# Separate buffers for block 2's background norms, their sums issued late, and GpSimd's weight remainders in four pieces

## The chip, the cores and the metric

The kernel runs on one core of a Trainium2 chip. The metric is device time in microseconds (us) for one launch, lower is better. A core has TensorE (matmuls and transposes, PE in the profile, its weight loads PEld), VectorE (DVE), ScalarE (ACT), GpSimd (POOL) and SyncE (SP, which here issues the weight transfers). Each runs its own list of instructions in order, and they wait for each other through semaphores.

## The reference

Two transformer blocks over 512 tokens of width 1024, all in fp32. Block 1 mixes forgetting attention with a gated spatial branch; block 2, where most of the change lies, mixes eight heads of chunked attention ("ca") with eight heads of latent attention ("mla"). Each has a convolutional feed-forward part. Cut to block 2's attention, it is:

```python
q = jnp.dot(rmsnorm_2(q_lat, g_q_latent[l]), w_q_up[l]).reshape(B, S, MLA_HEADS, MLA_QK)
kv = jnp.dot(rmsnorm_2(kv_lat, g_kv_latent[l]), w_kv_up[l]).reshape(B, S, MLA_HEADS, MLA_NOPE + MLA_V)
k_nope, v = kv[..., :MLA_NOPE], kv[..., MLA_NOPE:]
k = jnp.concatenate(
    [k_nope, jnp.broadcast_to(k_rope[:, :, None, :], (B, S, MLA_HEADS, MLA_ROPE))], axis=-1)
q = rmsnorm_2(q, g_mla_q[l])
k = rmsnorm_2(k, g_mla_k[l])
q = jnp.concatenate([q[..., :MLA_NOPE], rope(q[..., MLA_NOPE:], positions)], axis=-1)
k = jnp.concatenate([k[..., :MLA_NOPE], rope(k[..., MLA_NOPE:], positions)], axis=-1)
o_mla = mla_attention(q, k, v)
ca = ca_qkv.reshape(B, S, 3, CA_HEADS, CA_HEAD_DIM)
cq = rmsnorm_2(ca[:, :, 0], g_ca_q[l])
ck = rmsnorm_2(ca[:, :, 1], g_ca_k[l])
cv = ca[:, :, 2]
o_ca = chunk_attention(cq, ck, cv, rel_bias[l])
```

So per head and token, q and k of both kinds of attention are divided by the root of their mean square before the scores.

## The kernel before

**GEMMs.** Each fp32 product is made of three fp32r products: operands are split into a high part and a remainder. A weight slice of up to 128x1024 is loaded by `load_split` (L340): a transfer on SP's queue, a cast to the high part on ScalarE (`whi`, L350), and a subtraction that gives the remainder (`wlo`, L351). The subtraction is on VectorE, and on GpSimd for loads with `pool=True`: twelve 128x1024 slices, eight of them in block 1 (`w_u`, `w_qk`) and four in block 2 (`w_ck1`, `w_cv1`).

**Attention.** `attention()` (L619) goes through 64 strips in block 2, four per head, 16 heads: numbers 0 to 7 are ca heads, 8 to 15 mla heads. A strip is 128 queries. For each it issues the scores (TensorE), an add-min with the mask or bias `s`, which also takes the row minimum (VectorE, L597), the exponential `p` (ScalarE, L601), one strip later the transposes of `p` (TensorE, L610) with their copy `pt`, and another strip later the product with the values. Between these stand slices of GEMMs from a list of jobs, `fill`. The next heads' q and k are prepared up to five strips (`LEAD`) ahead: four transposes and a split for q, one strip later the same for k. For a ca head the transposes are at L1637 and the split products `qs`, `kh`, `kl` at L692 and below; for an mla head the transposes are at L1671 and the splits at L1675 to L1679.

**Background.** The norms are a second list, `bg`. They are generators that issue some instructions and yield a number of nanoseconds; `attention()` grants them 1700 ns a strip for the first 16 strips and 600 after that, and an unpaid debt stays for the next strip. `bg.upto(name)` issues all that is left up to a named job: `mla_head` (L1659) calls `bg.upto("mk1")` at head 12, the first that needs the second set of four mla heads. Jobs that matter here:

- `ca_norm(z, j)` (L1444): squares of four 128x256 slices of `ca` on GpSimd, their sums on VectorE (L1449), scale (L1455), power -1/2 on GpSimd (`rsqrt`, L526), four multiplies `ca` on VectorE (L1461).
- `m_squares` (L1534): for q or k of four heads the squares `sqm` of four column tiles on GpSimd (L1539) and their sums `nw` on VectorE (L1540). `q_norm(c)` goes on with a power and multiplies, then the rotary step (`rope`).
- `kr_rope` (L1566): square, copy and rotary step of the shared K part, on GpSimd.
- `k_norm(c)` (L1571): `m_squares`, adding the K part's sum (L1575), a scale (L1576), the power, and for each half `a` two multiplies of `mk` on GpSimd (L1582, L1584). Only then may TensorE transpose K for heads 8 to 11 (c = 0) or 12 to 15 (c = 1).

**What sets the order.** TensorE's order is written out by hand, as it is called above. The other engines' instructions are placed by a scheduler by priority; the background is issued with a lower priority (`BEHIND`), and `late()` (L528) puts an instruction after the current strip's add-min (`self.urgent`). Buffers also make work wait: pool `pp` has three buffers of 128x512, which the softmax strips `p` share with the background's squares and rotary intermediates; pool `stk2` has 12 for the heads' split q and k, four per mla head and three per ca head.

Of the kernel before, what the change touches and what calls it, by code (L numbers as in the profile page):

```python
# [10 lines left out]
F32 = mybir.dt.float32  # L11
# [4 lines left out]
ALU = mybir.AluOpType  # L16
AX = mybir.AxisListType
PSUM = bass.MemoryType.PSUM

P = 128  # L20
# [216 lines left out]
class Kernel:  # L237
# [99 lines left out]
    def load_split(self, src, pool, dest, skew):  # L337

        nc, n = self.nc, src.shape[-1]
        raw = self.wraw.tile([P, 1024], F32, tag="wraw", name="wraw")  # L340
        nc.sync.dma_start(out=raw[:, :n], in_=src)
        if dest:
            hi, lo = (self.pools[dest[0]].tile([P, 1024], F32R, tag=t, name="wsplit") for t in dest[1:])
        else:
            hi = self.whi.tile([P, 1088], F32R, tag="whi", name="whi")[:, skew:]
            lo = self.wlo.tile([P, 1088], F32R, tag="wlo", name="wlo")[:, skew:]
        with ExitStack() as ctx:
            for ins in self.before:
                ctx.enter_context(self.tc.issue_after(ins))
            nc.scalar.copy(hi[:, :n], raw[:, :n])  # L350
            (nc.gpsimd if pool else nc.vector).tensor_tensor(  # L351
                out=lo[:, :n], in0=raw[:, :n], in1=hi[:, :n].bitcast(F32), op=ALU.subtract)
        return hi, lo

    def prefetch(self, n):
# [957 lines left out]
    def rope_tables(self, tabs):  # L1313

        nc = self.nc
        t = self.pp.tile([P, 512], F32, tag="p", name="rope")
        ang, kf, kh = (t[:, 64 * j:64 * j + 64].rearrange("p (t f) -> p t f", f=16) for j in range(3))
        pf = t[:, 192:196]
        nc.vector.tensor_copy(pf, self.pos)
        for j in range(4):  # L1320
            nc.vector.tensor_scalar(out=ang[:, j], in0=self.row("inv"), scalar1=pf[:, j:j + 1],
                                    scalar2=None, op0=ALU.mult)
        magic = 12582912.0

        nc.vector.tensor_scalar(out=kf, in0=ang, scalar1=float(1 / (2 * np.pi)), scalar2=magic,
                                op0=ALU.mult, op1=ALU.add)
        nc.vector.tensor_scalar(out=kf, in0=kf, scalar1=magic, scalar2=None, op0=ALU.subtract)
        nc.vector.tensor_scalar(out=kh, in0=kf, scalar1=1.0 / 4096, scalar2=magic, op0=ALU.mult,
                                op1=ALU.add)
        nc.vector.tensor_scalar(out=kh, in0=kh, scalar1=magic, scalar2=4096.0, op0=ALU.subtract,  # L1330
                                op1=ALU.mult)
        nc.vector.tensor_tensor(out=kf, in0=kf, in1=kh, op=ALU.subtract)
        for part in TWO_PI_PARTS:
            for k in (kh, kf):
                nc.vector.scalar_tensor_tensor(out=ang, in0=k, scalar=-part, in1=ang, op0=ALU.mult,
                                               op1=ALU.add)
        lim = float(np.nextafter(np.float32(np.pi), np.float32(0)))
        nc.vector.tensor_scalar(out=ang, in0=ang, scalar1=lim, scalar2=-lim, op0=ALU.min, op1=ALU.max)
        cos, sin = (t[:, 256 + 64 * j:320 + 64 * j].rearrange("p (t f) -> p t f", f=16) for j in range(2))
        nc.scalar.activation(out=sin, in_=ang, func=AF.Sin)  # L1340

        half = float(np.pi / 2)
        nc.vector.tensor_scalar(out=kf, in0=ang, scalar1=half, scalar2=-2 * float(np.pi), op0=ALU.is_gt,
                                op1=ALU.mult)
        nc.vector.scalar_tensor_tensor(out=ang, in0=ang, scalar=half, in1=kf, op0=ALU.add, op1=ALU.add)
        nc.vector.tensor_scalar(out=ang, in0=ang, scalar1=lim, scalar2=-lim, op0=ALU.min, op1=ALU.max)
        nc.scalar.activation(out=cos, in_=ang, func=AF.Sin)
        for nm, tb in zip(("rope_gq", "rope_gk"), tabs):
            g = self.row(nm)
            for j, (src, lo) in enumerate(((cos, 0), (sin, 16), (cos, 16), (sin, 0))):  # L1350
                nc.vector.tensor_tensor(out=tb[:, j], in0=src,
                                        in1=g[:, lo:lo + 16].unsqueeze(1).to_broadcast([P, 4, 16]),
                                        op=ALU.mult)
# [11 lines left out]
    def block2_mix(self, xn, norm_b, final, evac, evac_last, norm_a):  # L1365
        nc, i = self.nc, self.i
        self.urgent = None
        ctx = ExitStack()
# [2 lines left out]
        self.att = self.pool("att2", 1, ctx=ctx)  # L1371
        one = self.pools["one"] = self.pool("one2", 1, ctx=ctx)
        two = self.pool("two2", 2, ctx=ctx)
        stk = self.pool("stk2", 12, ctx=ctx)
        tabq, tabk = tabs = [one.tile([P, 4, 4, 16], F32, name="tab" + z) for z in "qk"]

        gca = one.tile([P, 1], F32, name="gca")
# [1 line left out]
                                       in1=self.col("g_ca_k_2"), op0=ALU.mult, op1=ALU.mult)  # L1379
# [3 lines left out]
                                       in1=self.col("g_mla_k_2")[0:64], op0=ALU.mult, op1=ALU.mult)  # L1383
# [52 lines left out]
        ss = one.tile([P, 2, 2, 4, 4], F32, name="ssc")  # L1436
# [4 lines left out]
        def ca_slice(t, z, j):  # L1441
            return ca[t][:, z * 512 + 256 * j:z * 512 + 256 * (j + 1)]

        def ca_norm(z, j):  # L1444
            for t in range(4):
                v = ca_slice(t, z, j)
                sq = self.sm.tile([P, 256], F32, tag="sq", name="sqc", bufs=4)
                nc.gpsimd.tensor_tensor(out=sq, in0=v, in1=v, op=ALU.mult)
                nc.vector.tensor_reduce(out=ss[:, j, z, t], in_=sq.rearrange("p (g d) -> p g d", d=64),  # L1449
                                        axis=AX.X, op=ALU.add)  # L1450
                yield 400

            scale, eps = ((1.0, 64 * EPS), (1.0 / 64, EPS))[z]
            r = ss[:, j, z]
            nc.vector.tensor_scalar(out=r, in0=r, scalar1=scale, scalar2=eps, op0=ALU.mult, op1=ALU.add)  # L1455
            self.rsqrt(r)
            yield 1500
            for t in range(4):
                v3 = ca_slice(t, z, j).rearrange("p (g d) -> p g d", d=64)
                with self.late():  # L1460
                    nc.vector.tensor_tensor(out=v3, in0=v3, op=ALU.mult,  # L1461
                                            in1=ss[:, j, z, t].unsqueeze(2).to_broadcast([P, 4, 64]))
                yield 400
# [68 lines left out]
            return f  # L1532

        def m_squares(s2, src, d):  # L1534
            for t in range(4):
                sq = self.pp.tile([P, 512], F32, tag="p", name="sqm")[:, :4 * d]
                sq = sq.rearrange("p (h d) -> p h d", d=d)
                v = src[t // 2][:, t % 2, :, 0:d]
                nc.gpsimd.tensor_tensor(out=sq, in0=v, in1=v, op=ALU.mult)  # L1539
                nc.vector.tensor_reduce(out=s2[:, t], in_=sq, axis=AX.X, op=ALU.add)  # L1540
                yield 500

        def q_norm(c):

            r = small("r")
            yield from m_squares(r, mq[c], QK)
            nc.vector.tensor_scalar(out=r, in0=r, scalar1=1.0, scalar2=QK * EPS, op0=ALU.mult, op1=ALU.add)
            self.rsqrt(r)
            yield 1500
            for a in range(2):  # L1550
                v = mq[c][a]
                rq = r[:, 2 * a:2 * a + 2].unsqueeze(3)
                with self.late():
                    nc.vector.tensor_tensor(out=v, in0=v, in1=rq.to_broadcast([P, 2, 4, QK]), op=ALU.mult)
                rt = self.pp.tile([P, 4, 2, 4, 16], F32, tag="p", name="rt")
                self.rope(nc.vector if a else nc.gpsimd, v[:, :, :, 64:80], v[:, :, :, 80:96],
                          lambda j: tabq[:, j, 2 * a:2 * a + 2].unsqueeze(2).to_broadcast([P, 2, 4, 16]),
                          [rt[:, j] for j in range(4)])
                yield 1500

        def kr_rope():

            t = self.pp.tile([P, 4, 4, 32], F32, tag="p", name="krt")
            nc.gpsimd.tensor_tensor(out=t[:, 0], in0=kr, in1=kr, op=ALU.mult)
            nc.vector.tensor_reduce(out=krs, in_=t[:, 0], axis=AX.X, op=ALU.add)
            nc.gpsimd.tensor_copy(krr, kr)  # L1566
            tmp = self.pp.tile([P, 4, 4, 16], F32, tag="p", name="krt")
            self.rope(nc.gpsimd, krr[:, :, 0:16], krr[:, :, 16:32], lambda j: tabk[:, j],
                      [tmp[:, j] for j in range(4)])
            yield 600  # L1570
# [160 lines left out]
```

## Time and profile before

| | us |
|---|---|
| median of 3 runs | 1221.6 |
| lowest and highest | 1220.94, 1223.36 |
| profiled execution, its own time | 1219.78 |
| span of its instructions | 1218.0 |
| TensorE busy | 1194.5 (98%) |
| VectorE busy | 790.9 (65%) |
| ScalarE busy | 532.3 (44%) |
| GpSimd busy | 191.0 (16%) |

All durations come from the profiled execution, whose mean granted clock of TensorE is 0.996 of full speed. Between its span and its own time lie 1.78 us at the two ends. An engine's busy time says how much work it holds; what it costs the kernel is read from who waits for it. Block 2's attention runs from about 580 to 850 us.

### The profile page before, as it was taken

The numbers are of one execution on the slowest core, as the hardware profiler recorded it, in microseconds if no ns is written. First come the engines' busy times: TensorE is split into PE (matmuls) and PEld (weight loads), VectorE is DVE, ScalarE is ACT, GpSimd is POOL, SyncE is SP. The second block draws the span as 40 slices with busy tenths as digits, with TensorE's granted clock in tenths as the row PEclk, the third lists the DMA queues.
The fourth block names the chain that finished last, engine by engine and source line by source line (L and its number), as shares of the span: only waits on it lengthen the run. The fifth ranks groups of instructions, "written<-read, shape, count | busy, mean of one in ns | idle before, by whom it ended". The sixth has DMA issues, their size and how long they took to land.

```text
span 1218.0 us, 17371 instructions
## 1 busy us (share of the span) xinstructions
PE 1194.5 (98%) x6730; PEld 1041.3 (85%) x6730; DVE 790.9 (65%) x1402; ACT 532.3 (44%) x952; POOL 191.0 (16%) x209
## 2 busy tenths in 40 slices
PE   9999999999999999999998999999999999999998
PEld 6897888988888888888998998899988888888887
DVE  6657986698888886433666878876666565653221
ACT  6545554454444343222534556655544444442110
POOL 2367300300000000000244563301200000000000
PEclk9999999999999999999999999999999999999999
DMA  7322211266666666433122233111132222323330
GB/s 240 122 73 70 70 60 63 70 210 195 194 194 193 193 193 188 130 96 117 57 94 72 79 105 96 36 36 36 53 138 87 104 93 98 103 79 114 115 109 18
DMA packets 41313, 133.67 MB, mean 110 GB/s; under 512 B 4864, under 2 KB 5760, under 8 KB 41232
## 3 DMA queue, kind: packets, MB, share of 16 engines
q1 hardware_dynamic: 32816, 104.74, 27.0%
q10 hardware_dynamic: 8208, 27.27, 7.3%
q8 instruction: 52, 0.85, 0.3%
q0 software_dynamic: 208, 0.57, 0.2%
q14 instruction: 29, 0.24, 0.1%
HBM read 128.37 MB, written 2.10 MB: 107 GB/s over the span
## 4 chain that ended last, share of the span: by engine, by line
PE 85%; DVE 6%; POOL 4%; issue 2%; ACT 2%; DMA 1%; SPq 0%; ACTq 0%; POOLq 0%; DVEq 0%
PE mm L372 75%; PE s L372 4%; PE o L372 3%; PE s L610 2%; POOL wlo L351 1%; DVE nt L557 1%; DVE wlo L351 1%; DVE ca L1461 1%; DMA x<-in_xT_dram 1%; DVE s L597 1%; PE mm L1671 0%; PE s L732 0%; DMA cs<-in_c_dram 0%; ACT p L601 0%; DVE qs L693 0%
## 5 line engine op out<-in xcount | busy, mean ns | idle before, releaser
L351 DVE TENSOR_TENSOR wlo<-wraw,whi 128x1024 fp32r<-128x1024 f32 (+4 forms) x182 | 210.5, 1158 | 181.1 <-ACT whi L350 180.2
L350 ACT CAST whi<-wraw 128x1024 fp32r<-128x1024 f32 (+4 forms) x194 | 191.9, 992 | 278.4 <-PE mm L372 262.4
L372 PE MATMUL mm<-xnh,whi 128*128 128x512 f32 (+1 forms) x832 | 311.0, 374 | 1.2 <-DVE nt L557 0.6
L372 PE MATMUL mm<-xnl,whi 128*128 128x512 f32 (+1 forms) x832 | 309.8, 372 | 0.0
L372 PE MATMUL mm<-xnh,wlo 128*128 128x512 f32 (+1 forms) x832 | 309.7, 372 | 0.0
L372 PEld LDWEIGHTS mm<-xnh,whi 128*128 128x128 f32 x832 | 156.2, 188 | 28.5 <-PE mm L372 0.8
L372 PEld LDWEIGHTS mm<-xnh,wlo 128*128 128x128 f32 x832 | 156.2, 188 | 27.7
L372 PEld LDWEIGHTS mm<-xnl,whi 128*128 128x128 f32 x832 | 156.3, 188 | 26.7
L372 PE MATMUL mm<-gh,whi 128*128 128x512 f32 (+1 forms) x384 | 141.4, 368 | 1.1 <-DVE x L974 0.6
L372 PE MATMUL mm<-gh,wlo 128*128 128x512 f32 (+1 forms) x384 | 141.0, 367 | 0.0
L372 PE MATMUL mm<-gl,whi 128*128 128x512 f32 (+1 forms) x384 | 141.0, 367 | 0.0
L766 DVE SCALAR_TENSOR_TENSOR cv<-mm,cols,cv 128x510 f32<-128x510 f32 (+1 forms) x176 | 130.3, 745 | 2.5 <-ACT cv L764 0.5
L372 PE MATMUL mm<-whi,xnh 128*128 128x256 f32 (+3 forms) x304 | 97.9, 322 | 0.0
L372 PE MATMUL mm<-wlo,xnh 128*128 128x256 f32 (+3 forms) x304 | 94.1, 310 | 0.2 <-DVE wlo L351 0.2
L372 PE MATMUL mm<-whi,xnl 128*128 128x256 f32 (+3 forms) x304 | 94.0, 309 | 0.1
L372 PEld LDWEIGHTS mm<-gh,whi 128*128 128x128 f32 x384 | 72.1, 188 | 13.5 <-DVE x L974 0.8
L372 PEld LDWEIGHTS mm<-gl,whi 128*128 128x128 f32 x384 | 72.1, 188 | 12.1
L372 PEld LDWEIGHTS mm<-gh,wlo 128*128 128x128 f32 x384 | 72.1, 188 | 12.0
L1035 DVE CUSTOM_DVE_ANT_0 wada<-wada,cs,cols 128x1024 f32<-128x1024 f32 x48 | 61.5, 1282 | 27.4 <-DMA wada<-in_w_ada_dram 27.4
L601 ACT ACTIVATE p<-s,st 128x128 f32<-128x128 f32 (+1 forms) x96 | 50.7, 528 | 59.4 <-DVE st L597 58.0
L372 PE MATMUL mm<-mix,whi 128*128 128x256 f32 (+1 forms) x288 | 73.6, 344 | 1.5 <-DVE mix L752 0.9
L764 ACT ACTIVATE cv<-mm,cols 128x512 f32<-128x512 f32 x88 | 67.8, 775 | 0.1
(295 smaller groups left out, 1814.6 us busy)
## 6 DMA issues: line engine op xcount, KB each, us to landing
wraw<-in_w_up_dram SPq DMA_DIRECT2D x88, 512.0 KB, 3.5
wada<-in_w_ada_dram ACTq DMA_DIRECT2D x48, 512.0 KB, 3.7
wraw<-in_w_down_dram SPq DMA_DIRECT2D x32, 512.0 KB, 3.5
wraw<-in_w_out_dram SPq DMA_DIRECT2D x16, 512.0 KB, 3.5
wraw<-in_w_down_dram SPq DMA_DIRECT2D x16, 384.0 KB, 3.1
wraw<-in_w_qk_dram SPq DMA_DIRECT2D x8, 512.0 KB, 3.6
wraw<-in_w_v_dram SPq DMA_DIRECT2D x8, 256.0 KB, 5.0
x<-in_xT_dram SPq DMA_DIRECT2D x8, 256.0 KB, 6.3
```

The costliest lines, as they stand in the source:

```text
L350: nc.scalar.copy(hi[:, :n], raw[:, :n])
L351: (nc.gpsimd if pool else nc.vector).tensor_tensor(out=lo[:, :n], in0=raw[:, :n], in1=hi[:, :n].bitcast(F32), op=ALU.subtract)
L372: self.nc.tensor.matmul(out, lhsT, rhs, start=start, stop=stop, **kw)
L557: self.applied = nc.vector.scalar_tensor_tensor(out=t, in0=x[k][:, cs], scalar=gain(k), in1=r, op0=ALU.mult, op1=ALU.mult).ins
L597: self.urgent = nc.vector.tensor_tensor_reduce(out=s[:, cs], in0=s[:, cs], in1=b, scale=1.0, scalar=3e38 if j == 0 else st[:, j - 1:j], op ...
L601: nc.scalar.activation(out=p[:, :nk], in_=s[:, :nk], func=AF.Exp, bias=st[:, len(parts) - 1:len(parts)], scale=-1.0, accum_out=hd["sums"](qi))
L610: self.nc.tensor.transpose(s[:, c], p[:, c], self.ident)
L764: nc.scalar.activation(out=t, in_=ps, func=AF.Identity, scale=w[2], bias=self.col(cb, n))
L766: nc.vector.scalar_tensor_tensor(out=t[:, d:], in0=ps[:, :512 - d], scalar=w[2 - d], in1=t[:, d:], op0=ALU.mult, op1=ALU.add)
L1035: nc.vector.tensor_tensor_reduce(out=w, in0=w, in1=self.cs, scale=1.0, scalar=self.col("b_ada_2", n), op0=ALU.mult, op1=ALU.add, accum_out ...
L1461: nc.vector.tensor_tensor(out=v3, in0=v3, op=ALU.mult, in1=ss[:, j, z, t].unsqueeze(2).to_broadcast([P, 4, 64]))
```

## The change

Four things, the computed values being the same:

1. GpSimd's weight remainders are subtracted in pieces of 256 columns, so four instructions for each 128x1024 slice. VectorE's stay whole.
2. Background squares and rotary intermediates of block 2 go to a pool of their own, `bg2`, with two buffers; the stack pool shrinks from 12 to 10.
3. `ca_norm` issues its four squares first and then the four sums, late (after the strip's add-min).
4. `m_squares` issues the squares in pairs, yields 1700 after each pair (before: 500 after each square) and then issues the pair's two sums late.

```diff
-            (nc.gpsimd if pool else nc.vector).tensor_tensor(
-                out=lo[:, :n], in0=raw[:, :n], in1=hi[:, :n].bitcast(F32), op=ALU.subtract)
+            step = 256 if pool else n
+            for o in range(0, n, step):
+                c = slice(o, min(o + step, n))
+                (nc.gpsimd if pool else nc.vector).tensor_tensor(
+                    out=lo[:, c], in0=raw[:, c], in1=hi[:, c].bitcast(F32), op=ALU.subtract)
...
-        stk = self.pool("stk2", 12, ctx=ctx)
+        stk = self.pool("stk2", 10, ctx=ctx)
+        self.bgp = self.pool("bg2", 2, ctx=ctx)
...
         def ca_norm(z, j):
+            sqs = []
             for t in range(4):
                 v = ca_slice(t, z, j)
                 sq = self.sm.tile([P, 256], F32, tag="sq", name="sqc", bufs=4)
                 nc.gpsimd.tensor_tensor(out=sq, in0=v, in1=v, op=ALU.mult)
-                nc.vector.tensor_reduce(out=ss[:, j, z, t], in_=sq.rearrange("p (g d) -> p g d", d=64),
-                                        axis=AX.X, op=ALU.add)
+                sqs.append(sq)
                 yield 400
+            with self.late():
+                for t, sq in enumerate(sqs):
+                    nc.vector.tensor_reduce(out=ss[:, j, z, t], in_=sq.rearrange("p (g d) -> p g d", d=64),
+                                            axis=AX.X, op=ALU.add)
...
         def m_squares(s2, src, d):
+            sqs = []
             for t in range(4):
-                sq = self.pp.tile([P, 512], F32, tag="p", name="sqm")[:, :4 * d]
-                sq = sq.rearrange("p (h d) -> p h d", d=d)
+                sq = self.bgp.tile([P, 512], F32, tag="b", name="sqm")[:, :4 * d]
+                sqs.append(sq.rearrange("p (h d) -> p h d", d=d))
                 v = src[t // 2][:, t % 2, :, 0:d]
-                nc.gpsimd.tensor_tensor(out=sq, in0=v, in1=v, op=ALU.mult)
-                nc.vector.tensor_reduce(out=s2[:, t], in_=sq, axis=AX.X, op=ALU.add)
-                yield 500
+                nc.gpsimd.tensor_tensor(out=sqs[t], in0=v, in1=v, op=ALU.mult)
+                if t % 2:
+                    yield 1700
+                    with self.late():
+                        for j in (t - 1, t):
+                            nc.vector.tensor_reduce(out=s2[:, j], in_=sqs[j], axis=AX.X, op=ALU.add)
```

The tiles `rope`, `rt` and both `krt` move from `pp` to `bgp` in the same way. Line numbers of the changed kernel are 4 higher from L352 on (L601 is L597 of before), 9 and more in the norms (L1589 is L1576, L1650 is L1637, L1684 is L1671).

TensorE's list has the same instructions in the same order. The other engines' lists shift. Three places:

**VectorE, `k_norm(1)`.** `nw` are the sums of squares, `krs` the K part's sum, `lo` a split of q (L1676, L1689) or k (L1679, L1692), `s<-s,mlam` a strip's add-min. Before, from the k split of head 10:

```order
L1679 SCALAR_TENSOR_TENSOR lo<-mm,gml,hi 96x512
L961 SCALAR_TENSOR_TENSOR x_83<-mm,mod,x_83 128x512
L597 ISA s,st<-s,mlam 128x256
L597 ISA st 128x1
L1540 TENSOR_REDUCE nw<-sqm 128x4 x2
L1575 TENSOR_TENSOR nw<-nw,krs 128x16
L1576 TENSOR_SCALAR nw<-nw 128x16
```

and with the change, from the strip's `mix` to the k split of head 12:

```order
L753 TENSOR_TENSOR mix<-s,mix 128x512
L1554 TENSOR_REDUCE nw<-sqm 128x4 x2
L1689 TENSOR_TENSOR lo<-mm,hi 96x512
L1588 TENSOR_TENSOR nw<-nw,krs 128x16
L601 ISA s,st<-s,mlam 128x128
L601 ISA st 128x1
L1589 TENSOR_SCALAR nw<-nw 128x16
L1692 SCALAR_TENSOR_TENSOR lo<-mm,gml,hi 96x512
```

The scale (L1576, now L1589), which stood between head 10's splits and head 11's, stands between the two splits of head 12.

**GpSimd, the first norms of ca.** `sqc` are squares for `ca_norm`, `ssc` its power, `krt` and `krr` the rotary step of the K part. Before:

```order
L1430 TENSOR_TENSOR lath<-lat,lath 128x512
L1448 TENSOR_TENSOR sqc<-ca 128x256
L1566 COPY krr<-kr 128x128
L526 TENSOR_TENSOR ssc<-ssc,nhalf 128x16
L351 TENSOR_TENSOR wlo<-wraw,whi 128x1024 x2
L1448 TENSOR_TENSOR sqc<-ca 128x256 x4
```

and with the change:

```order
L1577 TENSOR_TENSOR krt<-kr 128x128
L1579 COPY krr<-kr 128x128
L1362 TENSOR_TENSOR krt<-krr,tabk 128x4x16
L1363 TENSOR_TENSOR krt<-krr,tabk 128x4x16
L1364 TENSOR_TENSOR krt<-krr,tabk 128x4x16
L1365 TENSOR_TENSOR krt<-krr,tabk 128x4x16
L1366 TENSOR_TENSOR krr<-krt 128x4x16
L1367 TENSOR_TENSOR krr<-krt 128x4x16
L530 TENSOR_TENSOR ssc<-ssc,nhalf 128x16
L355 TENSOR_TENSOR wlo<-wraw,whi 128x256 x8
L1454 TENSOR_TENSOR sqc<-ca 128x256 x4
```

The K part's square and rotary step, which came later, now precede this power, and the two remainders behind it are eight pieces.

**GpSimd, a later ca norm.** Before:

```order
L1448 TENSOR_TENSOR sqc<-ca 128x256 x2
L351 TENSOR_TENSOR wlo<-wraw,whi 128x1024
L526 TENSOR_TENSOR ssc<-ssc,nhalf 128x16
L351 TENSOR_TENSOR wlo<-wraw,whi 128x1024
L1564 TENSOR_TENSOR krt<-kr 128x128
```

and with the change:

```order
L1454 TENSOR_TENSOR sqc<-ca 128x256 x2
L355 TENSOR_TENSOR wlo<-wraw,whi 128x256 x4
L1549 TENSOR_TENSOR sqm<-mqk 128x384 x2
L530 TENSOR_TENSOR ssc<-ssc,nhalf 128x16
L355 TENSOR_TENSOR wlo<-wraw,whi 128x256 x4
```

Two squares `sqm` of the mla q part now stand ahead of the power, and `krt` behind it is gone.

## Rows read from the trace of the kernel before

**Rows 1.** Page, busy time, share and instructions of each engine

```profile
PE 1194.5 (98%) x6730; PEld 1041.3 (85%) x6730; DVE 790.9 (65%) x1402; ACT 532.3 (44%) x952; POOL 191.0 (16%) x209
```

**Rows 2.** TensorE's waits, 560 to 880 us: engine, line, waited for, us, times, longest

```profile
PE mm L1637 <- DVE ca L1461: 3.4, 2, 2.2
PE mm L1637 <- DVE qs L693: 2.9, 2, 2.6
PE s L610 <- ACT p L601: 0.9, 2, 0.7
```

**Rows 3.** Busy time by stretch (us): span, engines, clock, DMA share, GB/s

```profile
640.00:660.00 20.00, 16.39 (x122) 15.61 (x122) 12.33 (x18) 7.30 (x12) 10.54 (x6) 0.91 0.24 65
780.00:800.00 20.00, 20.00 (x147) 18.34 (x146) 14.16 (x33) 12.36 (x33) 0.58 (x2) 1.00 0.08 27
```

**Rows 4.** Timeline of TensorE, 785 to 788 us: start, duration, engine, line, operation

```profile
785.11 0.39 PE L372 MATMUL s<-hi,lo 96*128 96x512 f32 x1
...
786.79 0.28 PE L372 MATMUL s<-hi,lo 96*128 96x256 f32 x1
786.91 0.60 PE L1671 MATMUL mm<-ident,mqk 128*96 128x128 f32 x4
```

**Rows 5.** Timeline of VectorE, 773 to 775 us, end of the late K norm's sums

```profile
773.15 0.74 DVE L1540 TENSOR_REDUCE nw<-sqm 128x4 f32<-128x256 f32 x2
...
774.14 0.18 DVE L1576 TENSOR_SCALAR nw<-nw 128x16 f32<-128x16 f32 x1
```

**Rows 6.** Timeline of GpSimd, 774 to 781 us, the late K norm's power and multiplies

```profile
774.39 2.91 POOL L526 TENSOR_TENSOR nw<-nw,nhalf 128x16 f32<-128x16 f32 x1 [1.90 <-DVE nw L1576]
...
778.38 0.62 POOL L1584 TENSOR_TENSOR mqk<-krr,nw 128x256 f32<-128x256 f32 x1
...
779.96 0.62 POOL L1584 TENSOR_TENSOR mqk<-krr,nw 128x256 f32<-128x256 f32 x1
```

**Rows 7.** Timeline of VectorE, 785 to 788 us, head 12's splits

```profile
785.24 0.69 DVE L749 TENSOR_TENSOR mix<-s,mix 128x512 fp32r<-128x512 f32 x1 [1.25 <-ACT mix L748]
785.85 0.69 DVE L597 CUSTOM_DVE_ANT_0 s<-s,mlam 128x512 f32<-128x512 f32 x1
...
786.59 0.69 DVE L1676 TENSOR_TENSOR lo<-mm,hi 96x512 fp32r<-96x512 f32 x1
787.20 0.28 DVE L597 CUSTOM_DVE_ANT_0 s<-s,mlam 128x128 f32<-128x128 f32 x1
787.40 0.14 DVE L597 DVE_READ_ACCUMULATOR2_ANT st<- 128x1 f32 x1
```

**Rows 8.** Timeline of VectorE, 628 and 646 us, `ca` multiplies alone and beside remainders

```profile
628.29 1.43 DVE L1461 TENSOR_TENSOR ca<-ca,ssc 128x256 f32<-128x256 f32 x4 [2.88 <-POOL ssc L526]
...
646.06 5.81 DVE L1461 TENSOR_TENSOR ca<-ca,ssc 128x256 f32<-128x256 f32 x4 [3.02 <-POOL ssc L526]
```

**Rows 9.** Timeline of GpSimd, 646 to 700 us

```profile
646.08 5.17 POOL L351 TENSOR_TENSOR wlo<-wraw,whi 128x1024 fp32r<-128x1024 f32 x2
...
691.60 2.90 POOL L526 TENSOR_TENSOR ssc<-ssc,nhalf 128x16 f32<-128x16 f32 x1
...
699.09 0.31 POOL L1361 TENSOR_TENSOR krt<-krr,tabk 128x64 f32<-128x64 f32 x1
```

**Rows 10.** Timeline of TensorE, 651 and 702 us, the two stalls; bracket: idle before

```profile
651.60 1.50 PE L1637 MATMUL mm<-ident,ca 128*128 128x128 f32 x6 [2.17 <-DVE ca L1461]
...
701.91 0.63 PE L1637 MATMUL mm<-ident,ca 128*128 128x128 f32 x4 [2.65 <-DVE qs L693]
```

**Rows 11.** Timeline of TensorE at 116 and of GpSimd at 121 us, block 1

```profile
115.94 0.63 PE L732 MATMUL s<-ident,att 128*128 128x128 f32 x4 [1.77 <-DVE att L724]
...
121.47 1.13 POOL L1119 TENSOR_SCALAR gelu<-gelu 128x256 f32<-128x256 f32 x2
```

**Rows 12.** GpSimd by line and shape, 100 to 122 us: busy us, mean ns

```profile
L351 POOL TENSOR_TENSOR wlo<-wraw,whi 128x1024 fp32r<-128x1024 f32 x4 | 9.8, 2453 | 2.9 <-ACT whi L350 2.9
...
L1118 POOL TENSOR_TENSOR gelu<-uv 128x256 f32<-128x256 f32 x2 | 1.2, 614 | 0.0
```

More of the change, by code (lines that the diff above doesn't have):

```diff
@@ L1315, in rope_tables @@
         nc = self.nc
-        t = self.pp.tile([P, 512], F32, tag="p", name="rope")
+        t = self.bgp.tile([P, 512], F32, tag="b", name="rope")
         ang, kf, kh = (t[:, 64 * j:64 * j + 64].rearrange("p (t f) -> p t f", f=16) for j in range(3))
@@ L1554, in q_norm @@
                     nc.vector.tensor_tensor(out=v, in0=v, in1=rq.to_broadcast([P, 2, 4, QK]), op=ALU.mult)
-                rt = self.pp.tile([P, 4, 2, 4, 16], F32, tag="p", name="rt")
+                rt = self.bgp.tile([P, 4, 2, 4, 16], F32, tag="b", name="rt")
                 self.rope(nc.vector if a else nc.gpsimd, v[:, :, :, 64:80], v[:, :, :, 80:96],
@@ L1561, in kr_rope @@
         def kr_rope():
-            t = self.pp.tile([P, 4, 4, 32], F32, tag="p", name="krt")
+            t = self.bgp.tile([P, 4, 4, 32], F32, tag="b", name="krt")
             nc.gpsimd.tensor_tensor(out=t[:, 0], in0=kr, in1=kr, op=ALU.mult)
@@ L1566, in kr_rope @@
             nc.gpsimd.tensor_copy(krr, kr)
-            tmp = self.pp.tile([P, 4, 4, 16], F32, tag="p", name="krt")
+            tmp = self.bgp.tile([P, 4, 4, 32], F32, tag="b", name="krt")[:, :, :, 0:16]
             self.rope(nc.gpsimd, krr[:, :, 0:16], krr[:, :, 16:32], lambda j: tabk[:, j],
```

## The prediction

> **What bounds the kernel now.** I read the busy shares first: TensorE is busy for 1194.5 of the span's 1218.0 us [rows 1]. It is the bound, and its order of instructions is the same before and after the change. So the time can move only by TensorE's waits, 23.5 us in all, and by its clock. The waits of TensorE come next: in block 2's attention two pairs carry most, 3.4 us for the chunked-attention multiply `ca` and 2.9 us for the head's q product `qs`, both in front of transposes (L1637), then 0.9 us for a softmax strip [rows 2]. The table by stretches gives the clock: 0.91 in the 20 us that hold the first pair, which is a stretch of the lower of the two levels (1.2 instead of 2.4 GHz), and 1.00 from 780 to 800, where TensorE was busy for all 20.00 us [rows 3]. A stall there would be new. I therefore followed that place through TensorE, VectorE and GpSimd [rows 4 to 7], and the two present stalls through the same engines [rows 8 to 10].
>
> **The late K norm.** The change's longer yields make `k_norm(1)` fall behind its budget: before, `m_squares` gave 4 x 500 ns, now 2 x 1700, and a strip of the last 48 grants 600. `mla_head(4)` (the thirteenth head, number 12) then forces what is left of it, late reductions included. VectorE's order shows the result: before, the scale of the sums (L1576) stood after head 10's splits; now it stands after strip 44's add-min, right ahead of head 12's own K split. Before, it began at 774.14 [rows 5]; GpSimd's power and its four multiplies ended at 778.38 + 0.62 = 779.00 for the first two column tiles and 779.96 + 0.62 = 780.58 for the last two [rows 6], that is 4.86 and 6.44 us after it. TensorE transposes K of head 12 at 786.91 [rows 4], so it had 6.3 us to spare.
>
> Now VectorE walks this list, with durations of before [rows 5, 7]. TensorE's scores of strip 43 end at 785.50; the add-min of strip 43 ends at 786.20 and its read at 786.29; `mix` (0.69) ends about 786.9, two reductions (0.74 together) 787.6, the q split (0.60 from start to start) 788.2, the sum with the rotary part (taken as the scale's 0.18) 788.4, strip 44's add-min and read (0.34) 788.75. Only then the scale starts, since the order is fixed. The last two column tiles are ready at 788.75 + 6.44 + 0.1 for hand-over = 795.3, where TensorE would have issued them at about 787.15. Loss: **8.1 us**. It is seen as two waits, near 6.8 us (ready at 788.75 + 4.86 + 0.1 = 793.7 against 786.91) and 1.4 us. Bounds: strip 44's scores end at 787.07 [rows 4] and the scale stands behind their add-min, so it cannot start before 787.4, which gives 6.8; if VectorE loses another microsecond to ports, 9.1. Nothing hides it: behind the transposes TensorE's queue is closed, and it was busy for all of the following stretch [rows 3], so there is no idle time in which it could catch up.
>
> **The clock behind it.** After the present 2.17 us wait [rows 10] the clock dropped, and the 20 us read 0.91 [rows 3], so 0.09 x 20 = **1.8 us** of full-speed work went. A wait three times as long gets the same term; bounds 0, if the work behind it runs at the full level, and 3.6, twice the row.
>
> **The first present stall.** Before, two whole remainders followed GpSimd's power at 646.08, 5.17 us together; VectorE's four `ca` multiplies, from 646.06 on, took 5.81 us beside them, where alone they took 1.43 [rows 8, 9]. Each multiply waited for one whole 128x1024 subtraction. In pieces, a multiply waits for 0.6 us at most (128x256 on GpSimd: 0.61 [rows 12]), so four take 1.43 to 3.8. But the rotary work on the K part (`kr_rope`: a square and six 128x64 operations at 0.31 [rows 9], about 2.2 us) now stands ahead of that power. They start at 646.06 + 2.2 = 648.26, and the last ends 1.43 to 3.8 later, at 649.7 to 652.05 instead of 651.87: from -2.2 to +0.2, and I take the middle, **-1.0**.
>
> **The second present stall.** TensorE waits 2.65 us at 701.91 for `qs` [rows 10], behind a power at 691.60 and four `ca` multiplies. GpSimd's order now puts the squares of two 128x384 tiles ahead of the power, at 1.5 times the 0.61 of 128x256 [rows 12] 1.84 us, and takes `kr_rope` out from behind it, which frees VectorE of one reduction (0.37, half of the pair in [rows 5]). I take 1.84 - 0.37, about **+1.5**; bounds +1.9 and, if the whole wait were freed by ports, -2.65.
>
> **Small ones.** The 0.7 us wait of a strip's transposes [rows 2] came from an add-min that stood behind a rotary step waiting for GpSimd; the add-min now stands ahead: **-0.7**. In block 1, TensorE waits 1.77 us at 115.94 [rows 11] beside 128x1024 remainders of `w_u`. The pieces should release VectorE there; but GpSimd has no gap to give back, four remainders of 2.45 and the work between them [rows 12] lead to its last step at 121.47 [rows 11], on which VectorE's gelu product waits. A wait removed at 115.94 then returns in front of the next pair of strips: **0**, with -2.8 (1.77 and the 1 us behind it gone) and +0.6 (one piece's delay) as ends. The two stack buffers fewer cost nothing while their reuse lies behind a head's last strip; the two new background buffers stop squares from waiting for softmax strips, all of it off TensorE's path.
>
> On the price of a piece, the rows have 0.614 us for one 128x256 operation with two inputs, so four make 2.46, against 2.45 for one of 128x1024 [rows 12]: no extra. [...]
>
> **Sum.** 8.1 + 1.8 - 1.0 + 1.5 - 0.7 + 0 = +9.7 us on the profiled execution's 1219.78, so 1229.5. The median of the runs is 1221.6, 1.8 us above the profiled one. Carried over: **1231.3 us**.
>
> **Rivals.**
> - *The K norm stays covered.* VectorE would have to reach the scale by 786.91 - 4.96 = 781.95 (first tiles) and 787.15 - 6.54 = 780.6 (last). For it: the squares themselves come early, and before there were 6.3 us to spare. Against it: the scale stands behind an add-min whose scores end at 787.07. Then only -1.0 + 1.5 - 0.7 = -0.2 is left: 1221.4. Chance 0.06.
> - *Faster: the pieces free the shared work of VectorE and GpSimd everywhere.* The price is what a whole remainder holds up: 2.8 in block 1, 2.2 at the first stall, 2.65 at the second, 0.7 at the third, together 8.3 us, and 1213.3 with the K norm covered. It decides the sign only if the new K wait is under 8.3, and that wait has a lower bound of 6.8 by the order. With it at 6.8 and no clock loss the time would still be 1220.1; so faster needs the norm covered or all ends at once. Chance 0.05.
> - *The ten stack buffers bind.* A head takes four of them five strips ahead; if ScalarE's split must wait for an earlier head's last scores, each of the eight last heads could lose up to the length of a strip's scores and split, some 0.28 to 0.6 us [rows 4, 7], so 2 to 5 us on top: 1233.5 to 1236. Against it: the order has each reuse behind the last reader. Chance 0.07.
> - *The change does less than written:* the longer yields are eaten because the background has idle budget, and the norm lands where it was. The order excludes this.
>
> **How the numbers follow.** The forecast has 0.82. Its own range is 1225 to 1234.5: the ends of K wait and clock (-3.1, +2.8) and of the second stall and block 1 (-4.2 and -2.8 downwards, little upwards) do not all fall on one side. The third rival pulls the upper end to 1235.5; the first two, 0.11, are left out below: range 1224.8 to 1235.5. About 0.2% or 2.4 us is what a measurement here can tell from no change. Slower by more has the forecast and the third rival, 0.89 less 0.02 for the low ends: 0.87; within 0.2% the first rival and those ends: 0.08; faster 0.05.
>
> **What would show it.** The waits of TensorE after the change should have a new first line: transposes of L1684 for GpSimd's multiply (L1597), two times, some 8 us, with the power starting near 790 and the granted clock below 1.00 in the stretch behind it. The first `ca` multiplies should take 1.4 to 3.8 us for four instead of 5.81, and the wait before the L1650 transposes near 650 shrink by a microsecond, the one near 702 grow. It is wrong if the scale of `k_norm(1)` starts before 781 us, if the L1684 wait is under 5 us, or if block 1 ends more than 2 us earlier.

## The result and the profile after

The changed kernel takes 1235.93 us in the median of four runs (1235.48 to 1237.59), the kernel before in the same comparison 1222.48: a ratio of 1.011, 95% interval 1.009 to 1.0129, about 13.4 us slower. The forecast was slower by 9.7, to 1231.3, with 1235.5 as the upper end, so the time lies 0.4 beyond it. The direction and the main place were right, the sum was some 4 us short.

The page of the changed kernel, its busy times:

```profile
PE 1198.2 (97%) x6730; PEld 1043.4 (85%) x6730; DVE 781.8 (63%) x1404; ACT 532.7 (43%) x950; POOL 197.3 (16%) x245
```

TensorE is again the bound, with 1233.4 - 1198.2 = 35.2 us idle where it had 23.5 [rows 1]. Its waits, over the whole span:

```profile
PE mm L1684 <- POOL mqk L1597: 6.5, 2, 5.6
PE s L614 <- ACT p L605: 5.6, 7, 1.4
PE mm L1650 <- DVE qs L697: 4.8, 2, 4.5
PE mm L1650 <- DVE ca L1470: 1.6, 3, 0.6
PE mm L376 <- DVE kf L1197: 1.4, 1, 1.4
PE mm L376 <- ACT mqk L1539: 1.2, 1, 1.2
PE mm L1650 <- ACT whi L350: 1.1, 1, 1.1
```

The new first line is the one forecast: K transposes (L1684) for GpSimd's multiply (L1597), two times. `qs` is 4.8 instead of 2.9 and `ca` 1.6 instead of 3.4, which answers to [rows 2]; but the 1.1 for `whi` in the last line stands in front of the same transposes as `ca`, so that stall falls to 2.7. A strip's exponential now stands at 5.6 in seven waits, 2.4 of it before 150 us and 1.4 near 829. Lines for `kf` and for the K evacuation `mqk` (L1539) are new. The stretches, as in [rows 3]:

```profile
640.00:660.00 20.00, 17.00 (x125) 16.09 (x124) 10.24 (x17) 6.86 (x11) 15.99 (x21) 0.91 0.28 81
780.00:800.00 20.00, 13.03 (x86) 11.22 (x85) 9.24 (x28) 8.07 (x23) 7.28 (x7) 0.86 0.00 1
800.00:820.00 20.00, 20.00 (x132) 18.20 (x131) 12.85 (x30) 10.99 (x28) 0.00 (x0) 0.89 0.08 27
```

The clock reads 0.86 and then 0.89. Full speed reads 1.00 and the lower level 0.50, so that is (0.28 + 0.22) x 20 = 10 us at the lower level, where the stretch of the first stall has 0.18 x 20 = 3.6 in either kernel.

TensorE issues the same instructions in the same order in every kernel here, so each of its matmuls can be paired with the same one of the kernel before. The difference of their starts is the lag. Where it changes, time goes or comes:

| place, by the time in the kernel before | lag behind it, us | change | forecast |
|---|---|---|---|
| block 1, to 210 us | 2.0 | +2.0 | 0 |
| first ca stall, 650 | 1.7 | -0.4 | -1.0 |
| second ca stall, 702 | 3.7 | +2.0 | +1.5 |
| strip wait, 718 | 2.7 | -0.9 | -0.7 |
| K evacuation, 734 | 4.2 | +1.4 | none |
| small waits, 762 to 766 | 3.5 | -0.6 | none |
| head 12's K transposes, 787 | 11.3 | +7.8 | +8.1 |
| the clock behind them | 14.1 | +2.8 | +1.8 |
| head 15's strip, 813 | 15.5 | +1.4 | none |
| end | 15.1 | -0.4 | none |

Of block 1's 2.0 us, 0.5 is there by 10 us, before any piece. The lag at the end is 1.7 us more than the medians lie apart. Lags under 0.6 us, and steps of up to 2 us where the low level of the clock falls in a stretch of one profile and not of the other (near 120 and 596 us in some runs below), tell nothing.

**Head 12.** The rows that answer to [rows 4 to 7], on VectorE, GpSimd and TensorE:

```profile
789.19 0.70 DVE L601 CUSTOM_DVE_ANT_0 s<-s,mlam 128x512 f32<-128x512 f32 x1 [1.66 <-PE s L376]
...
790.40 0.74 DVE L1554 TENSOR_REDUCE nw<-sqm 128x4 f32<-128x256 f32 x2
791.06 0.68 DVE L1689 TENSOR_TENSOR lo<-mm,hi 96x512 fp32r<-96x512 f32 x1
...
791.74 0.29 DVE L601 CUSTOM_DVE_ANT_0 s<-s,mlam 128x128 f32<-128x128 f32 x1
...
791.95 0.16 DVE L1589 TENSOR_SCALAR nw<-nw 128x16 f32<-128x16 f32 x1
```

```profile
785.47 1.18 POOL L1549 TENSOR_TENSOR sqm<-mqk 128x256 f32<-128x256 f32 x2 [6.60 <-DVE nw L1554]
792.19 2.91 POOL L530 TENSOR_TENSOR nw<-nw,nhalf 128x16 f32<-128x16 f32 x1 [5.54 <-DVE nw L1589]
...
796.18 0.61 POOL L1597 TENSOR_TENSOR mqk<-krr,nw 128x256 f32<-128x256 f32 x1
...
797.75 0.61 POOL L1597 TENSOR_TENSOR mqk<-krr,nw 128x256 f32<-128x256 f32 x1
```

```profile
788.65 0.39 PE L376 MATMUL s<-hi,lo 96*128 96x512 f32 x1
...
796.85 0.66 PE L1684 MATMUL mm<-ident,mqk 128*96 128x128 f32 x2 [5.62 <-POOL mqk L1597]
798.42 0.66 PE L1684 MATMUL mm<-ident,mqk 128*96 128x128 f32 x2 [0.91 <-POOL mqk L1597]
798.73 1.20 PE L376 MATMUL mm<-mix,whi 128*128 128x512 f32 x2
```

VectorE walks the list of the forecast: the scale starts at 791.95, right after strip 44's add-min, 2.91 us after strip 43's scores end (788.65 + 0.39 = 789.04); 3.25 had been worked out. The last squares were done at 785.47 + 1.18 = 786.65; it is the sums' place that is late. The last multiply ends at 798.36, 6.41 after the scale (6.44 before), and the transposes wait 5.62 and 0.91. Behind them two matmuls take 1.20 us where the same pair took 0.71 in the kernel before.

### The profile page after: what moved, and what is told of

Same layout as the page of the kernel before. It is cut to its first block, busy times and chain, and to the rows that moved or that the text cites. A ratio compares the mean times of both kernels' runs of the same rounds, so it can differ in the third digit from the quotient of the medians.

```text
span 1233.4 us, 17397 instructions
## 1 busy us (share of the span) xinstructions
PE 1198.2 (97%) x6730; PEld 1043.4 (85%) x6730; DVE 781.8 (63%) x1404; ACT 532.7 (43%) x950; POOL 197.3 (16%) x245
## 4 chain that ended last, share of the span: by engine, by line
PE 84%; DVE 6%; POOL 5%; ACT 2%; issue 2%; DMA 1%; SPq 0%; POOLq 0%; ACTq 0%; DVEq 0%
PE mm L376 73%; PE s L376 4%; PE o L376 3%; PE s L614 2%; POOL wlo L355 1%; POOL ssc L530 1%; DVE nt L561 1%; DVE ca L1470 1%; DMA x<-in_xT_dram 1%; DVE wlo L355 1%; DVE s L601 1%; PE mm L1684 0%; ACT p L605 0%; ACT whi L350 0%; DVE qs L697 0%
```

## The experiments

Each kernel is compared with the kernel before, on the same chip. A lag is again TensorE's, from one profile of each.

### GpSimd's remainders in pieces

First the pieces alone, on the kernel before; then twice as many; then the changed kernel without them.

```diff
+            step = 256 if pool else n        # 128 in the second; n in the third
+            for o in range(0, n, step):
```

> Before, with only GpSimd's remainders cut into pieces of 256 columns. Theory: block 1's +2 us is the price of the pieces, since four of them take 2.8 to 3.0 us on GpSimd where one whole remainder took 2.4, and GpSimd has no gap there; so TensorE reaches the strip transposes near 138 us 2.0 to 2.4 us later than before. In block 2 the four ca multiplies at the first stall take 3.8 instead of 5.8 us, so that wait shrinks by 1.5 to 2. The sum is near 0: 1221 to 1224. Rival (my forecast): pieces cost GpSimd nothing, block 1 comes out even, and the time falls by 1.5 to 3 us, to 1219.5 to 1221.

> Before, with GpSimd's remainders in pieces of 128 columns, twice as many as in the first run. Theory: each further GpSimd instruction costs 0.1 to 0.16 us of its own (four pieces alone took 2.8 us, one whole 2.4), so eight take 3.2 to 3.5 us alone, 0.4 to 0.45 us from one start to the next, and TensorE reaches the transposes near 138 us 3.5 to 5 us later than before: 1223.5 to 1227. Rival: the price is VectorE getting in between the pieces, not the instruction; then pieces alone go at 0.35 us, eight take 2.8, and block 1 comes out as with four pieces, +2.

> The changed kernel with GpSimd's remainders whole again. Theory: block 1 comes back to the kernel before (2.0 to 2.4 us less at 140 us); at the first ca stall the four multiplies take 5 us or more again behind a power that is now later, so that stall grows by 2 to 3 us; the rest stays: 1234 to 1237. Rival: the 2 us of block 1 are chance; then they stay and the time is 1237 to 1239.

| kernel | median, us | ratio to before, 95% interval | lag at 210 us |
|---|---|---|---|
| before with pieces of 256 | 1222.9 | 1.0017 (1.0000 to 1.0034) | +1.5 |
| before with pieces of 128 | 1229.68 | 1.0069 (1.0044 to 1.0095) | +5.2 |
| changed, whole remainders | 1235.6 | 1.0117 (1.0092 to 1.0143) | -1.1 to changed |

The same remainder of block 1, near 68 us, in GpSimd's timelines, each near the shortest of its kind: whole in the kernel before, in four and in eight pieces.

```profile
67.20 2.40 POOL L351 TENSOR_TENSOR wlo<-wraw,whi 128x1024 fp32r<-128x1024 f32 x1 [1.08 <-ACT whi L350]
```

```profile
67.17 2.84 POOL L354 TENSOR_TENSOR wlo<-wraw,whi 128x256 fp32r<-128x256 f32 x4 [0.66 <-ACT whi L350]
```

```profile
67.99 3.39 POOL L354 TENSOR_TENSOR wlo<-wraw,whi 128x128 fp32r<-128x128 f32 x8
```

2.40, 2.84 and 3.39 us: three more instructions cost 0.44, seven 0.99, so each costs 0.14 to 0.15 us. The rival, that VectorE gets in between, is out for this part. It adds to the price elsewhere: at the first ca stall of the changed kernel, pieces between two `ca` multiplies take 0.92 us, and those behind them 0.74. GpSimd by line and shape in the changed kernel, 100 to 123 us, beside the row of `uv` times `gg_row` in the kernel before:

```profile
L355 POOL TENSOR_TENSOR wlo<-wraw,whi 128x256 fp32r<-128x256 f32 x16 | 11.9, 773 | 2.9 <-ACT whi L350 2.9
...
L1122 POOL TENSOR_TENSOR gelu<-uv 128x256 f32<-128x256 f32 x1 | 0.6, 612 | 0.0
```

```profile
L1145 POOL TENSOR_TENSOR uv<-uv,gg_row 128x256 f32<-128x256 f32 x4 | 3.1, 776 | 0.4 <-DVE uv L1143 0.4
```

Four remainders take 11.9 us instead of 9.8 [rows 12], which is 2.1 more on an engine without gaps (the twelve further instructions make 1.7 to 1.8 of it), and its gelu step of [rows 11] starts at 123.82 instead of 121.47. VectorE was indeed released, and TensorE reached the transposes of 115.94 early by 1.9 us in the first of these runs. But VectorE then stands idle until GpSimd's gelu step is done, here for 5.09 us where it was 1.14 in the kernel before:

```profile
123.72 0.42 DVE L1124 TENSOR_TENSOR gelu<-gelu,uv 128x256 f32<-128x256 f32 x1 [5.09 <-POOL gelu L1122]
```

TensorE waits for `kf`, `pt` and `p` behind it and is 1.9 late from 142 us on, 1.5 at 210. The whole remainders of the third run give 1.1 us back there, or 1.9 if the 0.8 is set aside by which this profile's lag is the larger near 30 us.

In block 2 the same pieces helped a wait and uncovered the next: in the first run the wait for `ca` falls from 3.4 to 0.9 us, and the scores behind it then wait for the transfer of `kh`.

```profile
PE mm L1640 <- DVE qs L696: 3.4, 2, 3.1
PE s L375 <- DMA kh<-kh: 2.1, 1, 2.1
PE mm L1640 <- DVE ca L1464: 0.9, 2, 0.5
```

The lag of this run ends at 3.5 us, 2.0 more than behind block 1, so the pieces gave nothing in sum. The second run's time is 2.7 us above the 1227 that was its upper end: in block 2 it loses 5.3 us more, with waits of 4.0 us for the transfer of `kh` and 6.1 for `qs`.

In the third run the `ca` wait is back at 4.9, and it eats the gain of block 1: no change in time, as expected.

### The late sums of the mla norms

```diff
+                if t % 2:
+                    yield 1700          # alone on the kernel before; then 1000, in the changed kernel
+                    with self.late():
+                        for j in (t - 1, t):
+                            nc.vector.tensor_reduce(out=s2[:, j], in_=sqs[j], axis=AX.X, op=ALU.add)
```

> Before, with only m_squares changed (squares in pairs, 1700 ns granted per pair, sums late), buffers still from the shared pool. Theory: this alone makes the K norm of head 12 late: TensorE waits 6 to 8 us for GpSimd's multiplies there, a stretch of lower clock of 10 us follows, 1230 to 1235. Rival: the two buffers of the new pool hold the squares back; then no wait over 1 us for GpSimd's multiplies here, and 1221 to 1224.

> The changed kernel with 1000 instead of 1700 ns granted per pair of squares, 2000 in all as before. Theory: the scale of the K norm for head 12 stands one head earlier in VectorE's order, its multiplies end before TensorE's transposes or less than 1.5 us after, the stretch of lower clock of 10 us there is gone or no longer than 3.4 us, and the time is 1224 to 1228. Rival: late sums in pairs are enough to make the norm late; then a wait of 4 us or more for GpSimd's multiplies stays, 1231 or more.

Alone, it takes 1227.25 us, ratio 1.0056 (1.0038 to 1.0074), 3 us less than expected. The wait is there, with the buffers shared as before, so the new pool's two buffers are not its cause:

```profile
PE mm L1675 <- POOL mqk L1588: 6.6, 2, 5.7
```

```profile
780.00:800.00 20.00, 13.37 (x76) 11.51 (x75) 8.48 (x22) 7.30 (x18) 7.32 (x7) 0.74 0.00 0
800.00:820.00 20.00, 20.00 (x146) 18.20 (x144) 14.76 (x35) 12.21 (x31) 0.00 (x0) 1.00 0.09 27
```

The lag rises by 7.3 us at head 12 and by 2.4 with the clock behind it. What I had left out is that the same edit also removes waits ahead of it, near 718 and 764 (-1.5 us together).

With 1000 ns the changed kernel takes 1230.94, ratio 1.0077 (1.0048 to 1.0107), 5 us under the median of the changed one; the two intervals overlap a little. GpSimd's last multiply ends at 789.37 + 0.61 = 789.98, and TensorE goes through without a wait and at the full clock:

```profile
783.81 2.91 POOL L530 TENSOR_TENSOR nw<-nw,nhalf 128x16 f32<-128x16 f32 x1 [2.96 <-DVE nw L1589]
...
789.37 0.61 POOL L1597 TENSOR_TENSOR mqk<-krr,nw 128x256 f32<-128x256 f32 x1
```

```profile
780.00:800.00 20.00, 20.00 (x144) 18.18 (x144) 14.38 (x36) 12.08 (x32) 6.95 (x7) 1.00 0.08 27
```

So the place was right: the 700 ns decide. From 605 to 804 us its lag grows by 1.7 us, where that of the changed kernel grows by 12.0; the wait for the K evacuation at 734 is gone as well. The total is less, and the forecast of 1224 to 1228 missed, since TensorE waits 2.5 us for a square of block 2's next norm (`sq`, L500) near 860 us, with a stretch of low clock behind it. The square itself is not late: it starts at 860.26, which is 853.08 of the kernel before plus the lag of 7.2, and there TensorE did not wait for it. Why it does here stays open.

### The late sums of the ca norms

```diff
-                nc.vector.tensor_reduce(out=ss[:, j, z, t], ...)
+            with self.late():           # alone on the kernel before; then taken back in the changed kernel
+                for t, sq in enumerate(sqs):
+                    nc.vector.tensor_reduce(out=ss[:, j, z, t], ...)
```

> Before, with only ca_norm's sums moved behind its four squares and late. Theory: a power on GpSimd comes later at one or two of the ca norms, so the waits before the ca transposes near 650 and 702 us change by 1 us at most each; 1221.5 to 1224. Rival: this is what makes the second stall 2 us longer; then the wait near 702 grows from 2.65 to 4 us or more, and the time is 1223.5 to 1226.

> The changed kernel with ca_norm's sums back behind each square, not late. Theory: the sums are what made the second stall longer; without them the power starts 3 us earlier and the wait near 702 us falls from 4.5 to 1.5 us or less: 1232 to 1234.5. Rival (my forecast): the two squares of the mla q part ahead of the power did it, or GpSimd's pieces did; then the wait stays over 3.5 us and the time at 1235 to 1237.

Alone: 1225.34 us, ratio 1.0027 (1.0012 to 1.0042). The rival holds. VectorE's and GpSimd's timelines and the wait:

```profile
693.38 1.40 DVE L1454 TENSOR_REDUCE ssc<-sqc 128x4 f32<-128x256 f32 x4
...
695.29 0.17 DVE L1459 TENSOR_SCALAR ssc<-ssc 128x16 f32<-128x16 f32 x1
...
698.47 4.07 DVE L1465 TENSOR_TENSOR ca<-ca,ssc 128x256 f32<-128x256 f32 x4 [0.29 <-POOL ssc L526]
```

```profile
695.54 2.90 POOL L526 TENSOR_TENSOR ssc<-ssc,nhalf 128x16 f32<-128x16 f32 x1 [1.69 <-DVE ssc L1459]
698.40 2.40 POOL L351 TENSOR_TENSOR wlo<-wraw,whi 128x1024 fp32r<-128x1024 f32 x1
```

```profile
PE mm L1641 <- DVE qs L693: 5.4, 2, 5.1
```

Four sums stand behind the add-min of a later strip, the scale starts at 695.29, and the power at 695.54 instead of 691.60 [rows 9], which less the lag of 1.2 is 2.7 us later. No mla squares are ahead of it here. The `ca` multiplies then begin together with a whole remainder and take 4.07 us instead of 2.01. Of the 5.4 us, 5.1 is one wait.

Taken back in the changed kernel: 1234.49, ratio 1.0106 (1.0087 to 1.0124). The power starts at 692.56, but the wait falls only from 4.5 to 3.3, not under 1.5: the multiplies then stand behind `mix` in VectorE's list, from 697.62 on, and take 3.06 us beside squares and pieces. Neither expectation of the wait held. So the late sums are a part of the longer second stall in the changed kernel, and what the multiplies then meet on GpSimd is likely another; no run takes that away alone.

### The buffers

```diff
-        stk = self.pool("stk2", 12, ctx=ctx)
+        stk = self.pool("stk2", 10, ctx=ctx)     # with the new pool alone, on the kernel before; then 11, in the changed kernel
+        self.bgp = self.pool("bg2", 2, ctx=ctx)
```

> Before, with only the background's own pool of two buffers and ten stack buffers instead of twelve. Theory: no wait for the K norm of head 12; ScalarE's split for K of head 15 waits for strip 55's scores, and TensorE then waits 1 to 1.5 us for that strip's exponential; 1222 to 1225. Rival (buffers hold the norm back): a wait of 5 us or more for GpSimd's multiplies, 1229 or more. If ten stack buffers bind at every mla head, several waits of 0.5 us and more from head 10 on, 1225 to 1228.

> The changed kernel with eleven stack buffers instead of ten. Theory: ScalarE's split for K of head 15 no longer waits for the scores of strip 55, TensorE's wait of 1.4 us for that strip's exponential goes, nothing else moves: 1234 to 1235.5. Rival: that wait comes from something else; then it stays and so does the time, 1235.5 to 1237.

TensorE's waits from 800 us on, in the first and from 815 us on in the second:

```profile
PE s L610 <- ACT p L601: 1.4, 1, 1.4
```

```profile
PE s L614 <- ACT p L605: 0.3, 1, 0.3
```

With ten stack buffers the strip of head 15 waits 1.4 us for its exponential, with eleven 0.3, as in the expectation: ScalarE's split (L1691) starts only when strip 55's scores have read their buffer, the subtraction and that strip's add-min stand behind it on VectorE. The step in the lag there falls from 1.4 to 0.3 us. Eleven give 1235.12 us, ratio 1.0109 (1.0082 to 1.0135), so the times of runs cannot tell it from the changed kernel; the trace does.

The pool alone takes 1227.28, ratio 1.0053 (1.0036 to 1.0070), above the 1222 to 1225 expected. Its norm of head 12 is on time. The time goes earlier, 2.3 us at the first ca stall, where `kr_rope` now stands ahead of the power and the remainders are whole (`ca` wait 4.9 instead of 3.4), and 3.7 at the second:

```profile
691.95 1.61 DVE L1456 TENSOR_SCALAR ssc<-ssc 128x16 f32<-128x16 f32 x1
697.36 0.55 DVE L1541 TENSOR_REDUCE nw<-sqm 128x4 f32<-128x384 f32 x1 [3.80 <-POOL sqm L1540]
697.83 0.68 DVE L724 TENSOR_TENSOR att<-o,sums 128x512 f32<-128x512 f32 x1
698.43 0.56 DVE L597 CUSTOM_DVE_ANT_0 s<-s,bs 128x384 f32<-128x384 f32 x1
```

With buffers of its own the mla square is issued earlier, behind a power on GpSimd, and its sum, not late here, blocks VectorE for 3.80 us with `att` and an add-min behind it. In the changed kernel, whose sums are late, VectorE has no such wait there. The four edits alone add up to 3.5 + 7.9 + 6.2 + 4.0 = 21.6 us of lag, and the whole to 15.1.

### A version that beats both

If whole remainders hold VectorE, VectorE may do them itself. On the kernel before:

```diff
-        fm("w_qk", [2, 6], pool=True)
-        fm("w_qk", [3, 7], pool=True)
+        fm("w_qk", [2, 6])
+        fm("w_qk", [3, 7])
```

In the second run also `w_ck1` and `w_cv1`, in the third `w_u` too.

> Before, with the four w_qk remainders of block 1 on VectorE instead of GpSimd (1.2 us each, four more). Theory: GpSimd's chain to its gelu step loses 9.8 us and VectorE is no longer held for whole remainders (8 us of it between 102 and 119 us), so the waits of 2.8 us near 116 go and the later ones do not come: block 1 is 2 to 3 us shorter, 1217.5 to 1220.5. Rival: VectorE becomes the bound there, with 4.8 us more work: block 1 comes out even or up to 3 us longer, 1220 to 1224.

> As the run before, and the four remainders of block 2 (w_ck1, w_cv1) on VectorE as well. Theory: the four ca multiplies at the first stall take 1.4 to 2 us instead of 5.8, but two remainders of 1.2 us stand on VectorE itself, so the two ca stalls shrink by 1 to 3 us in sum: 1215.5 to 1220. Rival: those remainders stand ahead of the ca multiplies and the transfer of kh is next in line, as in the first run, so nothing is won in block 2: within 1 us of the run before.

> Before, with all twelve of GpSimd's remainders on VectorE. Theory: w_u's four add 4.8 us of VectorE work from 62 to 85 us, where TensorE has not waited so far; the time is within 1 us of the run before. Rival: VectorE falls behind there and TensorE waits for a weight slice, 2 to 5 us longer than the run before.

| on VectorE | median, us | ratio to before, 95% interval |
|---|---|---|
| w_qk | 1216.96 | 0.9963 (0.9951 to 0.9976) |
| w_qk, w_ck1, w_cv1 | 1217.36 | 0.9972 (0.9957 to 0.9986) |
| all twelve | 1218.4 | 0.9975 (0.9959 to 0.9990) |

All three are faster than both kernels, by intervals that end below 1; among them no difference is shown. In the kernel before, the first of four multiplies `uv` on VectorE met a whole remainder on GpSimd and took 2.59 us, and the next two took 3.06:

```profile
108.31 2.59 DVE L1143 TENSOR_TENSOR uv<-uv,ss 128x256 f32<-128x256 f32 x1 [2.67 <-POOL ss L526]
```

```profile
108.24 2.38 POOL L351 TENSOR_TENSOR wlo<-wraw,whi 128x1024 fp32r<-128x1024 f32 x1
```

VectorE's timeline of the first of the three:

```profile
108.17 0.42 DVE L1143 TENSOR_TENSOR uv<-uv,ss 128x256 f32<-128x256 f32 x1 [2.54 <-POOL ss L526]
108.51 1.22 DVE L351 TENSOR_TENSOR wlo<-wraw,whi 128x1024 fp32r<-128x1024 f32 x1
...
111.45 0.75 DVE L1143 TENSOR_TENSOR uv<-uv,ss 128x256 f32<-128x256 f32 x2
```

It does four remainders of 1.2 us more (one shows 2.25, beside a GpSimd product) and is done sooner, and TensorE's waits of [rows 11] are gone: the lag falls by 1.9 and 1.2 us. That is 3.1 of the 4.2 us between the medians; where the rest comes from is not shown. Block 2's remainders on VectorE free the first `ca` stall (four multiplies in 1.43 us again) and TensorE then waits 3.0 us for `kl`, the next in line, so the rival held there.

## Where the prediction was right, and where it was not

The time lies 0.4 us above the range. What is short is mostly what the forecast had put at zero: block 1, the K evacuation and the strip of head 15, together 4.8 us.

**Right: the late K norm.** 8.1 us forecast, 7.8 measured, by the chain forecast. The edit alone reproduces it and 700 ns per pair less remove it. The small difference is VectorE's walk (2.91 instead of 3.25 us).

**Wrong: the price of a piece.** The step that failed is "no extra", and with it block 1 at 0 with +0.6 as its upper end; measured are +2.0, or +1.5 without the 0.5 that is there by 10 us, and +1.5 by the pieces alone. The row that it rested on (0.614 for 128x256 [rows 12]) is a tile times itself. A subtraction has two different tiles as its inputs, and the row of `uv` times `gg_row`, 0.776 in the same view, was the nearer one. That the second tile makes the difference is argued from such rows; no run isolates it. Squares have a fixed part too: 0.61 us for 256 columns and 0.83 for 384 leave some 0.17 for none. With the 0.14 to 0.15 us of the runs, three more instructions for each of four remainders would have been +1.7 to +1.8, and the sum 1233. The half of that step about the chain was right: VectorE was released and TensorE's wait came back further on. The remainders near 116 us are those of `w_qk`, and not of `w_u` as the forecast has it.

**Too small here: the clock.** The term was 1.8, from a row after a wait of 2.17 us. After 5.62 and 0.91 us of idle time the low level lasted 10 us by the stretches, and 2.8 us went once TensorE ran again; the bound of 3.6 held it. The size is that of one profile: with whole remainders, with eleven stack buffers and with the ca sums back, the same two waits come with some 7 us of low level (0.91 and 0.92 in the two stretches with eleven), and 1.5 to 1.7 us go.

**Near in size, wrong in cause: the second stall.** +1.5 was put down to two squares ahead of the power; +2.0 came. The ca sums alone, without those squares, make the wait 5.1 us instead of 2.65. In the changed kernel the power starts at 696.52, which less the lag of 1.7 is 0.5 us later than in that run less its 1.2: no more than this is left for the squares. The place of the sums had been read in VectorE's list, and not priced.

**Missed: two small waits.** The ten stack buffers bind, in one head and not in eight (+1.4). The rival had the right mechanism, and the forecast denied it altogether: "the order has each reuse behind the last reader", which holds in the list of each engine and does not say that the reader is done in time. And the K evacuation at 734 (+1.4): the scheduler put all four of its copies on ScalarE, three of them behind a weight cast, where two had been on VectorE. With 1000 ns one copy is on VectorE again and the wait is gone. In the run of the mla sums alone all four stand on ScalarE as well, but two come ahead of the cast, and TensorE loses nothing there. Why the scheduler placed them so was not tried.

**Near: the first stall.** -0.4 instead of -1.0. The multiplies fell from 5.81 to 3.58 us, inside the 1.43 to 3.8 of the forecast. They start at 649.90, which less the lag of 2.0 is 1.8 later than before (2.2 forecast), and end 0.4 earlier. The reading that each multiply had waited for a whole remainder is wrong: two of the four did (2.64 and 2.58 us), and the others took 0.43 and 0.41. In pieces all four take about 0.95.

**The rivals.** The K norm stayed late, and "faster" fell with it. The forecast gave that rival up to 8.3 us against a wait of at least 6.8, so the sign was not safe by these bounds. It came out safe because the pieces gave nothing in sum (ratio 1.0017 alone) and the wait came to 7.8.

## What to carry to other kernels

Price an instruction from a row of the same operation on the same kind of operands, and where it is cut in n, look for the fixed part: two sizes of one operation give it. Before an engine's operations are cut to free a port for another engine, see whether the other engine could do the work itself in the time that it stands blocked. A budget that delays background work is safe only as long as the work's consumer is further away than its whole chain, here 6.4 us behind the scale.

## What the runs showed of the hardware

A GpSimd subtraction of 128 rows costs 0.14 to 0.15 us per instruction beside its columns, 2.40, 2.84 and 3.39 us for one, four and eight pieces. A VectorE multiply that starts just behind a GpSimd subtraction waits for the whole of it: 2.59 us beside a whole remainder, 0.42 without, 0.95 beside pieces of 0.92. The Trainium skill ("SBUF — State Buffer", section "SBUF: two separate sides") has GpSimd and a VectorE operation with two inputs in SBUF share a pair of ports, which whichever starts first holds for its whole instruction; these rows agree. A power on 16 columns takes 2.9 us on GpSimd, longer than a subtraction of 1024 columns (2.40). TensorE's clock fell to its lower level behind one wait of 2.65 us [rows 10] (0.91 over 700 to 720 us of the kernel before). Behind the two waits at head 12 it stayed there for some 7 us in three profiles and 10 in two.
